# A two-layer decoder trunk: the modulation rows of the feed-forward stage go through GpSimd's DMA queue

## The chip, the cores and the metric

One core of one Trainium2 chip runs the whole kernel. The metric is device time in microseconds, as the median of several runs; beside it stands one execution taken with the hardware profiler. The engines are TensorE (PE, its weight loads PEld), VectorE (DVE), ScalarE (ACT), GpSimd (POOL) and SyncE (SP). SP does no arithmetic here: it issues DMA transfers, one after the other in a fixed order, and waits before each until its destination buffer is free.

## The reference

256 tokens of width 2048 pass through two layers. Each layer has a mixer (sliding-window attention beside an RWKV-7 recurrence, joined by one output projection) and a SwiGLU feed-forward, both with a modulation computed from a condition vector `c`:

```python
cond = jax.nn.silu(c)
for l in range(DEPTH):
    mod = (jnp.einsum('bd,de->be', cond, w_ada[l]) + b_ada[l]).reshape(B, N_MOD, 1, D_MODEL)
    sh_m, sc_m, gt_m, sh_f, sc_f, gt_f = [mod[:, i] for i in range(N_MOD)]
    u = x * (1 + sc_m) + sh_m
    ...
    mix = jnp.concatenate([y_attn, y_rwkv], axis=-1) @ w_out[l]
    x = layer_norm(DEEPNORM_ALPHA * x + gt_m * mix, ln1_w[l], ln1_b[l])
    u = x * (1 + sc_f) + sh_f
    gate, up = jnp.split(u @ w_gate_up[l], 2, axis=-1)
    ffn = (jax.nn.silu(gate) * up) @ w_down[l]
    x = layer_norm(DEEPNORM_ALPHA * x + gt_f * ffn, ln2_w[l], ln2_b[l])
```

All weights are float32 and are read from HBM once. `w_ada` is 2048 x 12288 per layer, `w_gate_up` 2048 x 11264 and `w_down` 5632 x 2048. The modulation is a product of one vector with a matrix, and does not depend on the tokens, so it can be computed at any time before its use.

## The kernel before, in words

**Weights.** `steps` brings the weights in chunks of 128 x 1024 floats (512 KB) into the tile `raw`, four buffers deep (L420 to L422). ScalarE rounds a chunk into `hi` (L430, three buffers), VectorE subtracts and gets the remainder `lo` (L431, two buffers). `stream` then multiplies each with TensorE, three products per block (L452, L453, L455), so that two reduced-precision parts give nearly full precision. A chunk of the feed-forward's main loop makes 12 matmuls of 512 columns.

**Modulation rows.** `ada_steps` computes 1024 values of one modulation. It reads 16 rows of blocks, 128 x 1024 floats each, into the tile `ast` (two buffers, L260 and L261), and VectorE multiplies each by a column of `cond` and adds it into `aacc` (L263 for the first, L265 for the others). Then two empty steps follow, and `ada_sums` adds over the partitions with eight TensorE transposes (L322) and ScalarE sums (L326). One such unit takes 19 steps; 20 units are to be done in a fixed list. Two of them go through another function, `ada_direct`, inside layer 0's mixer.

**How the two are interleaved.** After each chunk of weights `pump` adds `pace[0]` to a counter and takes a step of the list whenever the counter reaches one. In the feed-forward the pace is `AF_`, 0.75 steps a chunk in layer 0. `need` takes steps at once where a value is required. Each multiply of a row is ordered behind the low part of the chunk before it (`anchor`, L266 and L267). The order of the instructions within each engine is laid out when the kernel is built, from this program order and a model of durations, and then is fixed.

**Feed-forward.** `channel` first finishes the output projection and the first LayerNorm. From L1260 on it runs two rounds: gate and up for six (then five) blocks of 512 hidden columns, and the down projection of what these blocks made, added into `z`. After the second round come the second LayerNorm and, in layer 0, the start of the next layer's mixer. A LayerNorm's inverse root is a power on GpSimd (`rstd`, L1130). In the feed-forward GpSimd does nothing else. In the mixer it has small work of its own, and issues 32 transfers for a triangular inverse (L790 and L793).

All other transfers, weights and modulation rows alike, are issued by SP through `dma = nc.sync.dma_start`, apart from twelve issued by ScalarE.

Of the kernel before, what the change touches and what calls it, by code (L numbers as in the profile page):

```python
# [69 lines left out]
def hybrid_trunk_kernel(  # L70
# [8 lines left out]
    V, S, G, PE = nc.vector, nc.scalar, nc.gpsimd, nc.tensor  # L79
    dma = nc.sync.dma_start  # L80
# [170 lines left out]
    def ada_steps(l, mod, c0):  # L251

        src = w_ada[l].rearrange("(j p) n -> p j n", p=P)
        n0 = mod * D + c0
        if direct[0]:
            yield from ada_direct(l, mod, c0, src[:, :, n0:n0 + 1024])
            return
        acc = adap.tile([P, 1024], F32, tag="aacc", name="aacc")
        for j in range(KT):
            t = adap.tile([P, 1024], F32, tag="ast", name="ast", bufs=2)  # L260
            dma(t, src[:, j, n0:n0 + 1024])  # L261
            if j == 0:
                V.tensor_scalar_mul(acc, t, cond[:, 0:1])  # L263
            else:
                ins = V.scalar_tensor_tensor(acc, t, cond[:, j:j + 1], acc, ALU.mult, ALU.add)  # L265
                if anchor:  # L266
                    tc.add_manual_dep(ins.ins, anchor[0], order, reason="behind the weight stream")  # L267
            yield
        for _ in range(LAG):
            yield  # L270

        ada_sums(l, mod, c0, [acc[:, i * P:(i + 1) * P] for i in range(8)])
        done.add((l, mod, c0 // 1024))
        yield

    def ada_direct(l, mod, c0, src):

        gv = ps.tile([P, 512], F32, tag="m0", name="gv", bufs=1)
        turn[:] = 1, 0
        ahead = []  # L280

        def row_sums(j):
            t = ahead.pop(0)
            for q in range(4):
                PE.matmul(gv[32 * q:32 * q + 32, 0:T], lhsT=cond[:, j:j + 1].to_broadcast([P, 32]), rhs=t[:, q * T:(q + 1) * T],
                          start=(j == 0), stop=(j == KT - 1))

        for j in range(KT):
            if j >= LAG:
                row_sums(j - LAG)  # L290
            t = adap.tile([P, 1024], F32, tag="aacc", name="ast") if j % 3 == 2 else adap.tile([P, 1024], F32, tag="ast", name="ast", bufs=2)
            dma(t, src[:, j])
            ahead.append(t)
            yield
        for j in range(KT - LAG, KT):
            row_sums(j)
            yield
        row = adap.tile([P, T], F32, tag="aacc", name="grow")
        S.copy(row, gv[:, 0:T])
        turn[:] = 1, 1  # L300
        b = bank()
        for i in range(2):
            PE.transpose(b[:, i * P:(i + 1) * P], row[:, i * P:(i + 1) * P], ident)
        col = mod * KT + c0 // P
        bv = b[:, 0:T].rearrange("p (i q r) -> p q i r", q=4, r=32)
        V.scalar_tensor_tensor(mods[l][:, col:col + 8].rearrange("p (q i) -> p q i", q=4), bv[:, :, :, 0], 1.0 if mod in (1, 4) else 0.0,
                               prm(l, "b_ada", col, 8).rearrange("p (q i) -> p q i", q=4), ALU.add, ALU.add)
        done.add((l, mod, c0 // 1024))
        yield

    def ada_sums(l, mod, c0, blocks, idle=0):

        col = mod * KT + c0 // P
        n = len(blocks)
        sm = adap.tile([P, 8], F32, tag="asum", name="asum", bufs=2)
        for q in range(0, n, 4):
            b = bank()
            if q == 0:
                warm(b, idle)
            m = min(4, n - q)  # L320
            for i in range(m):
                PE.transpose(b[:, i * P:(i + 1) * P], blocks[q + i], ident)  # L322
            for i in range(m):
                bi = b[:, i * P:(i + 1) * P]
                if RED:
                    S.activation(bi, bi, AF.Copy, accum_out=sm[:, q + i:q + i + 1])  # L326
            if not RED:
                V.reduce_sum(sm[:, q:q + m], b[:, 0:m * P].rearrange("p (i k) -> p i k", k=P), axis=AX.X)
        V.scalar_tensor_tensor(mods[l][:, col:col + n], sm[:, 0:n], 1.0 if mod in (1, 4) else 0.0,
                               prm(l, "b_ada", col, n), ALU.add, ALU.add)  # L330
        if mod in (2, 5):
            row = adap.tile([8, P], F32, tag="arow", name="arow", bufs=2)[0:n]
            rb = bank()
            PE.transpose(rb[0:n, 0:P], mods[l][:, col:col + n], ident)
            S.copy(row, rb[0:n, 0:P])
            dma(gates[l, mod // 3, c0 // P:c0 // P + n], row)
# [23 lines left out]
    def ada_all(units):  # L360
        for l, m, h in units:
            yield from ada_steps(l, m, h * 1024)
# [10 lines left out]
                       + halves(1, 5))  # L373
    pace = [0.0, 0.0]
    anchor = []
    direct = [False]

    def pump():

# [101 lines left out]
    def cols(w, c0, width):  # L481
        wv = w.rearrange("(k p) n -> p k n", p=P)

        def f(rv, k0, m):
            return [(rv, wv[:, k0:k0 + m, c0:c0 + width])]
        return f
# [646 lines left out]
    def normalise(fp, z, t, stt):  # L1133
        mv, rs = rstd(fp, stt)
        V.scalar_tensor_tensor(rs[:, 1:2], mv[:, 0:1], -1.0, rs[:, 0:1], ALU.mult, ALU.mult)
        for q in range(4):
            zq = z[:, t, q * 512:(q + 1) * 512]
            if q % 2:
                S.activation(zq, zq, AF.Identity, scale=rs[:, 0:1], bias=rs[:, 1:2])
            else:  # L1140
                V.tensor_scalar(zq, zq, rs[:, 0:1], rs[:, 1:2], ALU.mult, ALU.add)
# [38 lines left out]
    def channel(l, ys, wa, fp):  # L1180
# [31 lines left out]
        for c0, w in ((1024, 512), (1536, 512)):  # L1212
            nq = w // 512
            bk = all_banks(nq)
            src, pieces = cols(w_out[l], c0, w), [(q * 512, 512) for q in range(nq)]
# [34 lines left out]
        def finish(t):  # L1250
            mv, rs = rstd(fp, stt[t])
            V.tensor_scalar_mul(mv[:, 0:1], mv[:, 0:1], -1.0)
            for q in range(4):
                o = q * 512
                zq = z[:, t, o:o + 512]
                V.scalar_tensor_tensor(zq, zq, mv[:, 0:1], lw[:, o:o + 512], ALU.add, ALU.mult)
                V.scalar_tensor_tensor(zq, zq, rs[:, 0:1], lb[:, o:o + 512], ALU.mult, ALU.add)
                dma(out[0, t * P:(t + 1) * P, o:o + 512], zq)

        gtf = fp.tile([P, D], F32, tag="gt", name="gtf")  # L1260
        wg = w_gate_up[l].rearrange("(k p) (s n) -> p k s n", p=P, s=2)
        first = True
        for lo_g, hi_g in ((0, 6), (6, 11)):
# [42 lines left out]
            for c0, w in ((0, 1024), (1024, 512), (1536, 512)):  # L1306
# [11 lines left out]
                for ts in ((0,), (1,)) if apart else ((0, 1),):  # L1318
# [5 lines left out]
                    for t in ts:  # L1324
# [8 lines left out]
                        if c0 == 1536 and not first:  # L1333
                            finish(t) if l + 1 == L else normalise(fp, z, t, stt[t])
            first = False
        if l + 1 == L:
            return None, None
        us = []
# [44 lines left out]
    for l in range(L):  # L1383
        pace[0] = AP[l]
        with tc.tile_pool(name=f"mix{l}", bufs=1, reuse_waits="tile") as mp:
            ys, wa = mixer(l, us, mp, feeds)
        pace[0] = AO[l]
        with tc.tile_pool(name=f"ffn{l}", bufs=1, reuse_waits="tile") as fp:
            us, feeds = channel(l, ys, wa, fp)
# [30 lines left out]
```

## Time and profile before

| | us |
|---|---|
| median of 3 runs | 2661.34 |
| lowest and highest run | 2660.47, 2666.17 |
| profiled execution | 2673.23 |
| its span, first to last instruction | 2671.2 |
| busy: PE, DVE, ACT, POOL | 2514.0, 1804.7, 1186.5, 146.7 |

The profiled execution is one more run, with the profiler on. Rows of the profile give an instruction's engine, source line, operation and tiles (`out<-in`), how often it occurs, and its time. A window's row gives each engine's busy time in that stretch, the clock that TensorE was granted (1.00 is full speed), the mean busy share of the 16 DMA engines, and the bytes moved. A wait's row says which instruction stood still for what, with the total, the number of times and the longest. The chain of waits follows the work that ended last back through what released it.

### The profile page before, as it was taken

What the parts mean: (1) busy time and instruction counts of PE and PEld (TensorE: products, weight loads), DVE (VectorE), ACT (ScalarE), POOL (GpSimd) and SP (SyncE); (2) the same over time, 40 slices, a digit from 0 to 9 for tenths busy, and PEclk for the clock granted to TensorE, in tenths of its full rate; (3) what the DMA queues carried; (4) which work ended last, traced back from release to release, by engine and by line L of the source; (5) the groups of instructions that cost most, each with busy time, mean ns of one, the idle gap of its engine ahead of it and who ended that gap; (6) DMA issues with size and microseconds to landing.
All of it is one profiled execution on the core that took longest, in us unless ns stands there. A gap on an engine that the chain in (4) does not pass through costs nothing.

```text
span 2671.2 us, 42267 instructions
## 1 busy us (share of the span) xinstructions
PE 2514.0 (94%) x15619; PEld 2090.1 (78%) x15619; DVE 1804.7 (68%) x2439; ACT 1186.5 (44%) x2023; POOL 146.7 (5%) x368
## 2 busy tenths in 40 slices
PE   3799998999999999999999998989899999999997
PEld 3697785677878888888788977867788888888887
DVE  7977766579877777677787776564855455545456
ACT  2464454435544444444454644543444443344442
POOL 1002212000000000000000024110000000000000
PEclk9899998999999999999999999988999999999999
DMA  9978658698998889888878785414655655566654
GB/s 371 358 215 253 202 176 266 207 335 301 327 328 303 309 301 317 284 299 304 293 247 291 218 264 148 129 50 179 221 189 184 195 184 196 195 190 188 191 189 149
DMA packets 336384, 637.51 MB, mean 239 GB/s; under 512 B 59510, under 2 KB 126514, under 8 KB 334642
## 3 DMA queue, kind: packets, MB, share of 16 engines
q1 hardware_dynamic: 333170, 629.05, 71.0%
q0 software_dynamic: 1280, 2.62, 0.4%
q10 hardware_dynamic: 1728, 3.15, 0.3%
q8 instruction: 122, 2.00, 0.3%
q14 instruction: 84, 0.69, 0.1%
HBM read 622.08 MB, written 12.62 MB: 238 GB/s over the span
## 4 chain that ended last, share of the span: by engine, by line
PE 62%; DMA 6%; DVE 5%; ACT 1%; issue 1%; POOL 0%; SPq 0%; DVEq 0%; ACTq 0%; POOLq 0%
PE acc L453 18%; PE acc L455 17%; PE acc L452 17%; DMA ast<-in_w_ada_dram 3%; DVE lo L431 2%; PE acc L465 1%; PE acc L466 1%; PE acc L464 1%; DMA raw<-in_w_gate_up_dram 1%; DVE aacc L265 1%; PE mb L1290 1%; DMA raw<-in_w_out_dram 1%; DMA raw<-in_w_in_dram 1%; PE mb L322 0%; DMA tm<-tinv 0%
## 5 line engine op out<-in xcount | busy, mean ns | idle before, releaser
L430 ACT CAST hi<-raw 128x1024 fp32r<-128x1024 f32 (+2 forms) x728 | 758.2, 1044 | 1093.2 <-PE acc L455 826.5
L431 DVE TENSOR_TENSOR lo<-raw,hi 128x1024 fp32r<-128x1024 f32 (+2 forms) x728 | 880.4, 1212 | 519.0 <-PE acc L453 350.1
L453 PE MATMUL acc<-lo,u 128*128 128x512 f32 x1568 | 515.7, 396 | 14.3 <-DVE lo L431 14.3
L455 PE MATMUL acc<-hi,u 128*128 128x512 f32 x1568 | 508.1, 392 | 0.0
L452 PE MATMUL acc<-hi,u 128*128 128x512 f32 x1568 | 460.1, 395 | 0.7 <-ACT u L410 0.7
L265 DVE SCALAR_TENSOR_TENSOR aacc<-ast,cond,aacc 128x1024 f32<-128x1024 f32 x270 | 345.7, 1280 | 105.8 <-DMA ast<-in_w_ada_dram 104.5
L453 PEld LDWEIGHTS acc<-lo,u 128*128 128x128 f32 x1568 | 294.2, 189 | 80.2 <-DVE lo L431 20.1
L452 PEld LDWEIGHTS acc<-hi,u 128*128 128x128 f32 x1568 | 296.3, 189 | 63.3 <-issue 1.2
L455 PEld LDWEIGHTS acc<-hi,u 128*128 128x128 f32 x1568 | 296.3, 189 | 61.9 <-issue 0.3
L453 PE MATMUL acc<-lo,ht 128*128 128x512 f32 (+1 forms) x720 | 243.7, 377 | 3.4 <-DVE lo L431 3.0
L455 PE MATMUL acc<-hi,ht 128*128 128x512 f32 (+1 forms) x720 | 242.2, 375 | 0.0
L452 PE MATMUL acc<-hi,ht 128*128 128x512 f32 (+1 forms) x720 | 217.1, 376 | 0.0
L464 PE MATMUL acc<-u,hi 128*128 128x256 f32 x720 | 201.1, 287 | 1.8 <-ACT hi L430 1.8
L465 PE MATMUL acc<-u,hi 128*128 128x256 f32 x720 | 201.3, 287 | 0.0
L466 PE MATMUL acc<-u,lo 128*128 128x256 f32 x720 | 188.7, 289 | 1.9 <-DVE lo L431 1.7
L453 PEld LDWEIGHTS acc<-lo,ht 128*128 128x128 f32 x720 | 135.1, 188 | 30.2 <-DVE lo L431 6.4
L455 PEld LDWEIGHTS acc<-hi,ht 128*128 128x128 f32 x720 | 135.6, 188 | 24.2
L452 PEld LDWEIGHTS acc<-hi,ht 128*128 128x128 f32 x720 | 134.8, 188 | 24.4
L464 PEld LDWEIGHTS acc<-u,hi 128*128 128x128 f32 x720 | 139.8, 194 | 4.5 <-ACT hi L430 2.0
L465 PEld LDWEIGHTS acc<-u,hi 128*128 128x128 f32 x720 | 139.6, 194 | 2.9 <-issue 1.6
L466 PEld LDWEIGHTS acc<-u,lo 128*128 128x128 f32 x720 | 130.7, 194 | 6.5 <-DVE lo L431 3.3
L1130 POOL TENSOR_TENSOR brs<-brs,mhalf 128x1 f32<-128x1 f32 x8 | 7.3, 916 | 1711.9 <-DVE brs L1129 776.6
(358 smaller groups left out, 2923.6 us busy)
## 6 DMA issues: line engine op xcount, KB each, us to landing
ast<-in_w_ada_dram SPq DMA_DIRECT2D x368, 512.0 KB
raw<-in_w_gate_up_dram SPq DMA_DIRECT2D x704, 256.0 KB
raw<-in_w_down_dram SPq DMA_DIRECT2D x176, 512.0 KB
raw<-in_w_in_dram SPq DMA_DIRECT2D x82, 512.0 KB
raw<-in_w_out_dram SPq DMA_DIRECT2D x64, 512.0 KB
raw<-in_w_in_dram SPq DMA_DIRECT2D x120, 256.0 KB
ast<-in_w_ada_dram SPq DMA_DIRECT2D x32, 256.0 KB
lnw<-in_ln_w_dram SPq DMA_DIRECT2D x4, 1024.0 KB
```

The costliest lines, as they stand in the source:

```text
L265: ins = V.scalar_tensor_tensor(acc, t, cond[:, j:j + 1], acc, ALU.mult, ALU.add)
L430: S.copy(h, fl)
L431: ins = V.tensor_tensor(r, fl, h.bitcast(F32), ALU.subtract)
L452: PE.matmul(bt, lhsT=xh, rhs=hi[:, c0:c0 + w], start=st, stop=False)
L453: PE.matmul(bt, lhsT=xh, rhs=lo[:, c0:c0 + w], start=False, stop=False)
L455: PE.matmul(banks[t][q][:, 0:w], lhsT=xl, rhs=hi[:, c0:c0 + w], start=False, stop=sp_)
L464: PE.matmul(bt, lhsT=hi[:, c0:c0 + w], rhs=xh, start=st and opens, stop=False)
L465: PE.matmul(bt, lhsT=hi[:, c0:c0 + w], rhs=xl, start=False, stop=False)
L466: PE.matmul(bt, lhsT=lo[:, c0:c0 + w], rhs=xh, start=False, stop=sp_ and closes)
L1130: G.tensor_tensor(rs[:, 0:1], rs[:, 0:1], mhalf[:, 0:1], ALU.pow)
L1290: PE.transpose(b[:, i * T + t * P:i * T + (t + 1) * P], hh[t][:, (2 * k2 + i) * P:(2 * k2 + i + 1) * P], ident)
```

## The change

A flag `quiet` is set just before the feed-forward's two rounds are laid out and is cleared after them. While it is set, `ada_steps` issues its transfers from GpSimd (`G.dma_start`) and not from SP. The transfers themselves, their buffers and all arithmetic stay the same, and so do the weights' issues. `ada_direct` and `ada_first` are not touched. The flag is set in both layers.

```diff
         for j in range(KT):
             t = adap.tile([P, 1024], F32, tag="ast", name="ast", bufs=2)
-            dma(t, src[:, j, n0:n0 + 1024])
+            (G.dma_start if quiet[0] else dma)(t, src[:, j, n0:n0 + 1024])
...
-    direct = [False]
+    direct, quiet = [False], [False]
...
         gtf = fp.tile([P, D], F32, tag="gt", name="gtf")
+        quiet[0] = True
         wg = w_gate_up[l].rearrange("(k p) (s n) -> p k s n", p=P, s=2)
...
             first = False
+        quiet[0] = False
         if l + 1 == L:
             return None, None
```

## The prediction, made before the change was run

> **What bounds the kernel now.** I read the page first, then the two feed-forward stages as windows, then the waits inside the first one, then its chain of waits and its timeline.
>
> ```profile
> span 2671.2 us, 42267 instructions
> ...
> q0 software_dynamic: 1280, 2.62, 0.4%
> ```
>
> The profiled execution took 2673.23 us, 2.0 us more than its span and 11.9 us (0.45%) more than the median of the runs shown, 2661.34 us. I make the sum as a difference on the profiled execution and put it on the median.
>
> ```profile
> 621.00:1381.50 760.50, 751.91 (x3494) 622.12 (x3495) 585.59 (x583) 345.03 (x532) 0.54 (x1) 1.00 0.89 306
> 1921.50:2657.50 736.00, 735.97 (x3400) 614.11 (x3400) 388.30 (x415) 308.25 (x347) 1.62 (x2) 1.00 0.58 185
> ```
>
> The columns are the stretch, its length, then the busy time and count of PE, PEld, DVE, ACT and POOL, the granted clock, the DMA share and GB/s. The first row is the feed-forward of layer 0, from its first gate matmul to its last down matmul; the second is the same work in layer 1. Both are PE's. Modulation rows run only in the first:
>
> ```profile
> L261 SPq DMA_DIRECT2D ast<-in_w_ada_dram x175: 327/328/750, 618.4 to 1378.0; - x175
> L265 DVE SCALAR_TENSOR_TENSOR aacc<-ast,cond,aacc x164: 1272/1280/1287, 617.1 to 1376.7; 128x1024 f32<-128x1024 f32 x164
> ```
>
> So 175 transfers change queue, all in layer 0; by layer 1's feed-forward no row is left. Layer 0's stage is 24.5 us longer. Part of that is TensorE's work for the row sums:
>
> ```profile
> L322 PE MATMUL mb<-ident,aacc x88: 271/272/273, 665.2 to 1366.9; 128*128 128x128 f32 x88
> ...
> 1366.15 1.03 PE L322 MATMUL mb<-ident,aacc 128*128 128x128 f32 x8
> ```
>
> Eleven groups of eight at 1.03 us are 11.3 us. What remains, 24.5 - 11.3 = 13.2 us, is what PE loses to late weights there. That is all that a better order of transfers can win: 0.5%.
>
> ```profile
> ACT hi L430 <- PE acc L455: 321.4, 195, 4.9
> DVE aacc L265 <- DMA ast<-in_w_ada_dram: 65.3, 48, 4.0
> DVE lo L431 <- PE acc L453: 48.5, 36, 2.3
> ...
> ACT hi L430 <- DMA raw<-in_w_gate_up_dram: 37.4, 18, 5.4
> ...
> ACT hi L430 <- DMA raw<-in_w_down_dram: 14.3, 6, 2.8
> ```
>
> These are the waits of layer 0's stage (total us, times, longest). VectorE makes the low parts of the weights and multiplies the rows, in one order fixed at build time. When a row is late, VectorE stands (65.3 us in 48 waits, 1.36 us each) and the next low part is late. How little reserve it has shows against layer 1, where the same wait for PE, VectorE being ahead, is 275.8 us and not 48.5:
>
> ```profile
> DVE lo L431 <- PE acc L453: 275.8, 187, 1.7
> ```
>
> **The change part by part.** First, SP loses 175 issues of 0.328 us, 57 us. The question is whether weights wait behind a row on SP.
>
> ```profile
> 1330.30 1.21 DVE L431 TENSOR_TENSOR lo<-raw,hi 128x1024 fp32r<-128x1024 f32 x1
> 1339.61 1.28 DVE L265 SCALAR_TENSOR_TENSOR aacc<-ast,cond,aacc 128x1024 f32<-128x1024 f32 x1
> 1343.35 1.29 DVE L265 SCALAR_TENSOR_TENSOR aacc<-ast,cond,aacc 128x1024 f32<-128x1024 f32 x1 [1.32 <-DMA ast<-in_w_ada_dram]
> ...
> 1331.54 0.37 SPq L422 DMA_DIRECT2D raw<-in_w_down_dram  x1
> 1337.99 0.34 SPq L261 DMA_DIRECT2D ast<-in_w_ada_dram  x1
> 1340.92 0.34 SPq L261 DMA_DIRECT2D ast<-in_w_ada_dram  x1
> ```
>
> A low part ends at 1331.51 and frees a raw buffer; SP issues the next weights at 1331.54. A row's multiply ends at 1340.89 and SP issues the next row at 1340.92. SP is a follower of VectorE: it sits in wait and reacts in 0.03 us.
>
> ```profile
> SPq L422 <- DVE lo L431: 291.6, 246, 3.7
> ```
>
> Its weights wait 291.6 us for low parts. Taking the rows off SP is worth nothing by this; were a weight issue really held up now and then, it is at most the 0.33 us of one row's issue.
>
> Second, POOL gains 175 issues. The kernel has transfers on that queue already, in the mixer:
>
> ```profile
> L793 POOL DMA_DIRECT2D tm<-tinv x16: 682/687/702, 237.6 to 1749.5; - x16
> ...
> tm<-tinv POOLq DMA_DIRECT2D x16, 128.0 KB, 3.6
> ```
>
> An issue takes 0.69 us there against 0.33 on SP, so 175 are 121 us of POOL, which does 0.54 us of other work in the stage. Hidden. What they are queued ahead of is the power (L1130) of the LayerNorm that closes the stage, with VectorE and then PE behind it: at worst one issue, 0.7 us, once. The sixteen issues lie within 682 to 702 ns, so nothing that VectorE does meanwhile holds them up.
>
> Third, and this is the term that counts, the landing of a row. A row's slot is freed by the multiply two rows back, and its transfer starts then. How long it takes now is seen where the chain runs through it:
>
> ```profile
> 735.95 6.39 DMA ast<-in_w_ada_dram
> ...
> 1095.51 4.91 DMA ast<-in_w_ada_dram
> ...
> 1337.99 5.26 DMA ast<-in_w_ada_dram
> ...
> 1344.66 5.45 DMA ast<-in_w_ada_dram
> ```
>
> The mean is 5.5 us. What time it has follows from PE's pace:
>
> ```profile
> 661.69 0.91 PE acc L452 x4
> 664.41 0.91 PE acc L452 x4
> ```
>
> One weight chunk is 2.72 us. At the pace of 0.75 there are three rows in four chunks, so two rows further is 5.44 us or 8.16 us, and less the 1.28 us of the multiply a transfer has 4.16 or 6.88 us. At 5.5 us the short third of them waits 1.34 us: 173 multiplies / 3 = 58 waits of 1.34 us, against the 48 of 1.36 us that the trace has. The model holds, and it has two edges: below 4.16 us no row waits, above 6.88 us every row does.
>
> Now the landing on POOL's queue. The only rows are the mixer's 128 KB transfers, under three loads of the DMA engines:
>
> ```profile
> L793 POOL DMA_DIRECT2D tm<-tinv x2: 687/688/690, 441.1 to 441.8; - x2
> DMA to landing us min/median/max: 4.8/5.2/5.5
> L793 POOL DMA_DIRECT2D tm<-tinv x2: 682/686/689, 1559.3 to 1560.0; - x2
> DMA to landing us min/median/max: 6.8/6.9/6.9
> L793 POOL DMA_DIRECT2D tm<-tinv x2: 687/688/690, 1677.8 to 1678.5; - x2
> DMA to landing us min/median/max: 3.1/3.1/3.1
> ...
> 441.00:447.00 6.00, 5.61 (x51) 2.92 (x50) 2.89 (x11) 1.23 (x4) 3.06 (x3) 1.00 1.04 283
> 1559.00:1567.00 8.00, 7.46 (x59) 6.74 (x57) 5.44 (x10) 6.54 (x18) 1.90 (x3) 1.00 0.99 278
> 1677.00:1682.00 5.00, 5.00 (x56) 4.68 (x56) 1.52 (x2) 2.49 (x9) 1.67 (x3) 1.00 0.45 133
> ```
>
> The second last number is the DMA share: 3.1 us at 0.45, 4.8 to 6.9 us at about 1. A queue of its own does not escape the load. A row has 512 KB; at the 391 GB/s that the trace reaches at its best,
>
> ```profile
> 50.00:100.00 50.00, 37.58 (x278) 35.17 (x279) 47.10 (x48) 17.02 (x35) 0.00 (x0) 0.91 1.05 391
> ```
>
> the other 384 KB add 1.0 us. So the ends for a row are 4.1 us (unloaded) and 7.9 us (loaded); the stage's share of 0.89 is nearest to the loaded rows, which give 5.8 to 7.9. I take 6.5, below their middle because those transfers are cut into pieces of 256 bytes and a row into pieces of 4 KB. That is 1.0 us more than now.
>
> Then the 48 waits become 2.36 us each, +48 us, and some of the 6.88 us rows start to wait; I put +10 us on them. VectorE idles in all 760.5 - 585.6 = 175 us of the stage, 65 of it in these waits, so +58 us fits on the average and reaches PE only where waits come in a bunch. Now 65.3 + 37.4 + 14.3 = 117 us of late data cost PE 13.2 us, a share of 0.11; as reserve shrinks the share grows, and I take 0.17: 58 x 0.17 = +10 us. Sum: 0 (SP) + 0 to 0.7 (POOL) + 10 = 2673 + 10 = 2683 us profiled, 2671 on the median.
>
> The order in which the build lays out each engine's instructions may shift with the queue, and no row shows this: -5 to +5 us, taken as 0.
>
> The Trainium skill (DMA: Bandwidth & Descriptors, section "Latency and other measured facts") gives about 1 us to the first byte for a transfer issued by GpSimd and about 0.6 us by SyncE; by that the landing grows by 0.4 us as an estimate, 48 x 0.4 x 0.17 = 3 us, and the sum would be 2665. The loaded rows say more, and I go by them.
>
> **The rivals.** (a) No change that can be told. A row lands at up to 6.0 us on the new queue, because large pieces suffer less than small ones. Then 48 x 0.5 x 0.17 = 4 us at most, and VectorE's idle time takes it: 2661 to 2665, say 2663. For it speak SP's reaction in 0.03 us (nothing to win) and the 175 us of idle VectorE; against it the 4.8 to 6.9 us under load.
>
> The Trainium skill has a rule for this rival (same page, "Issuing engines are not separate DMA queues"): transfers of all issuing engines run on the same 16 DMA engines, and another issuer only saves sequencer time. The trace agrees so far as that POOL's transfers slow down with the load of SP's.
>
> (b) Faster. On its own queue a row passes the weights already queued on SP's, and lands at the unloaded 4.1 us. Below 4.16 us no row waits: the 65.3 us go, more than half of the 117 us of late data, and PE regains 65.3 / 117 x 13.2 = 7 us, up to 13 with the weights' share: 2648 to 2654. It decides from about 4.7 us on down, where half of the waiting is gone. For it speaks that a row now takes 5.5 us where size alone is 1.3 us, much of it in line; against it, that POOL's own small transfers were not spared the line.
>
> (c) Much slower. The landing is above 6.88 us, as the pair at 1559 would give. All 173 rows wait, VectorE has no reserve and becomes the bound: two rows per landing plus 1.28 us. At 7.5 us that is 4.39 us a row against 3.63 at the pace; 173 x 0.76 = 131 us of waits, of which the 110 us of VectorE's other idle time hide most: +20 to +45 us, 2681 to 2706.
>
> **How the numbers follow.** Forecast (landing 6.0 to 6.9 us, +6 to +20 us) 0.35; (a) 0.33; (b) 0.20; (c) 0.12. Of 2661.34 us, 0.2% is 5.3 us, about what a measurement tells from no change. Faster 0.20 is (b), same 0.33 is (a), slower 0.47 is the forecast and (c). The range leaves out the better half of (b) and the worse half of (c): 2652 to 2692. The forecast's own is 2667 to 2681.
>
> **What would show it.** Right: in the changed kernel's layer 0 stage the wait of L265 for the row's transfer is 100 to 140 us and not 65; SP's weights still go out within 0.05 us of a low part's end; POOL shows some 121 us of issues; the stage is about 770 us long against 760.5; layer 1's feed-forward stays at 736.0. Wrong for (b): the wait of L265 falls under 30 us and the stage under 755. Wrong for (c): nearly all 164 multiplies wait and PE's share in the stage falls below 0.97. And if the stages outside layer 0's feed-forward move by more than 5 us, it was the order of instructions, which I took as 0.

## The result, and the profile after

The changed kernel takes 2685.73 us against 2660.90 us of the kernel before on the same chip (medians of six runs each): 0.9% slower, ratio 1.009, 95% interval 1.007 to 1.011. The forecast was 2671 us in a range of 2652 to 2692, slower as the likeliest side. The direction came as predicted, and so did the chain behind it (late rows, late low parts, TensorE waiting). Why the rows are late and how much of it reaches TensorE did not, and the loss of 24.8 us is about two and a half times the +10 us of the sum.

The profiled execution of the changed kernel took 2685.16 us. First the page: the span, and the queues, where q0 is the one that GpSimd's issues go to (packets, MB, share of 16 engines).

```profile
span 2683.2 us, 42302 instructions
...
q1 hardware_dynamic: 308546, 539.39, 60.5%
q0 software_dynamic: 25904, 92.29, 10.4%
...
L261 POOL DMA_DIRECT2D ast<-in_w_ada_dram x171 | 90.4, 529 | 667.7 <-DVE aacc L265 527.9
...
ast<-in_w_ada_dram POOLq DMA_DIRECT2D x171, 512.0 KB, 5.6
```

q0 carried 2.62 MB before and carries 92.29 MB now: 171 rows of 512 KB are 89.7 MB more. Four of the 175 rows in the stage are those of the steps behind it and stay with SyncE.

Now the two feed-forward stages as windows, between the same matmuls as before (same columns: stretch, length, PE, PEld, DVE, ACT, POOL, clock, DMA share, GB/s).

```profile
624.50:1397.70 773.20, 755.91 (x3494) 621.06 (x3495) 584.36 (x583) 345.95 (x532) 90.94 (x172) 1.00 0.87 301
1932.50:2669.00 736.50, 735.81 (x3400) 613.70 (x3400) 388.14 (x415) 308.17 (x347) 1.62 (x2) 1.00 0.58 186
```

Layer 0's stage has grown from 760.5 to 773.2 us; layer 1's stands at 736.5 against 736.0. Outside layer 0's stage the two spans are level: 2671.2 - 760.5 = 1910.7 us before, 2683.2 - 773.2 = 1910.0 us after. PE's idle time in the stage (length less busy) went from 8.6 to 17.3 us, and its busy time from 751.9 to 755.9 at the same number of matmuls. The waits inside that stage (total us, times, longest):

```profile
DVE aacc L265 <- DMA ast<-in_w_ada_dram: 87.8, 57, 4.4
DVE lo L431 <- PE acc L453: 45.9, 34, 2.3
ACT hi L430 <- DMA raw<-in_w_gate_up_dram: 44.0, 21, 5.0
...
PEld acc L453 <- DVE lo L431: 29.4, 31, 2.7
...
PE acc L453 <- DVE lo L431: 17.0, 23, 2.3
ACT hi L430 <- DMA raw<-in_w_down_dram: 10.9, 5, 2.3
```

Rows are waited for 87.8 us and no longer 65.3. What follows from it stands in the last rows: PE and its weight loads wait longer for low parts. The same two waits in the kernel before:

```profile
PEld acc L453 <- DVE lo L431: 15.7, 18, 2.1
...
PE acc L453 <- DVE lo L431: 8.2, 13, 1.7
```

The weight load's wait has grown by 29.4 - 15.7 = 13.7 us, the stage by 12.7 us.

How late a row is shows in the timeline of the changed kernel.

```profile
1323.06 1.23 DVE L431 TENSOR_TENSOR lo<-raw,hi 128x1024 fp32r<-128x1024 f32 x1 [1.50 <-PE acc L453]
1324.31 0.38 SPq L422 DMA_DIRECT2D raw<-in_w_down_dram  x1
...
1326.92 1.28 DVE L265 SCALAR_TENSOR_TENSOR aacc<-ast,cond,aacc 128x1024 f32<-128x1024 f32 x1
...
1328.50 0.53 POOL L261 DMA_DIRECT2D ast<-in_w_ada_dram  x1 [2.19 <-DVE aacc L265]
```

SyncE still sends the weights 0.02 us after the low part (1323.06 + 1.23 = 1324.29). A row's multiply ends at 1328.20; GpSimd's issue begins at 1328.50 and takes 0.53 us, so it is over 0.83 us after the buffer came free. On SyncE it was over after 0.37 us (0.03 and 0.34). Each row's issue is over 0.46 us later; how this divides into a later start and a longer issue rests on GpSimd's spans, which are rough in the profile. Counted from the start of the issue it lands as before:

```profile
L261 POOL DMA_DIRECT2D ast<-in_w_ada_dram x171: 527/527/617, 624.9 to 1377.4; - x171
DMA to landing us min/median/max: 3.8/5.6/8.0
```

The median of 5.6 us is hardly more than the 5.5 us that the chain showed on SyncE's queue.

### The profile page after: what moved, and what is told of

Its sections match the earlier page's. It is cut to its first block, busy times and chain, and to the rows that moved or that the text cites. A ratio compares the mean times of both kernels' runs of the same rounds, so it can differ in the third digit from the quotient of the medians.

```text
span 2683.2 us, 42302 instructions
## 1 busy us (share of the span) xinstructions
PE 2521.1 (94%) x15619; PEld 2092.7 (78%) x15619; DVE 1803.5 (67%) x2439; ACT 1187.0 (44%) x2023; POOL 236.8 (9%) x539
## 3 DMA queue, kind: packets, MB, share of 16 engines
q0 software_dynamic: 25904, 92.29, 10.4%
## 4 chain that ended last, share of the span: by engine, by line
PE 73%; DMA 12%; DVE 8%; issue 2%; ACT 2%; POOL 1%; SPq 0%; DVEq 0%; POOLq 0%; ACTq 0%
PE acc L453 19%; PE acc L455 18%; PE acc L452 18%; DMA ast<-in_w_ada_dram 7%; DVE lo L431 3%; PE acc L466 3%; PE acc L465 3%; PE acc L464 2%; DVE aacc L265 2%; DMA raw<-in_w_out_dram 1%; DMA raw<-in_w_gate_up_dram 1%; PE mb L322 1%; PE mb L1291 1%; DVE aacc L353 1%; DMA tm<-tinv 1%
## 5 line engine op out<-in xcount | busy, mean ns | idle before, releaser
L430 ACT CAST hi<-raw 128x1024 fp32r<-128x1024 f32 (+2 forms) x728 | 758.4, 1044 | 1091.0 <-PE acc L455 823.9
L431 DVE TENSOR_TENSOR lo<-raw,hi 128x1024 fp32r<-128x1024 f32 (+2 forms) x728 | 880.2, 1212 | 507.9 <-PE acc L453 346.1
L453 PE MATMUL acc<-lo,u 128*128 128x512 f32 x1568 | 516.5, 397 | 19.0 <-DVE lo L431 18.9
L453 PEld LDWEIGHTS acc<-lo,u 128*128 128x128 f32 x1568 | 292.8, 189 | 87.6 <-DVE lo L431 27.9
L453 PE MATMUL acc<-lo,ht 128*128 128x512 f32 (+1 forms) x720 | 245.2, 379 | 6.3 <-DVE lo L431 6.2
L453 PEld LDWEIGHTS acc<-lo,ht 128*128 128x128 f32 x720 | 135.2, 189 | 34.6 <-DVE lo L431 11.0
L261 POOL DMA_DIRECT2D ast<-in_w_ada_dram x171 | 90.4, 529 | 667.7 <-DVE aacc L265 527.9
```

Of the source, the lines that this page charges most:

```text
L261: (G.dma_start if quiet[0] else dma)(t, src[:, j, n0:n0 + 1024])
L430: S.copy(h, fl)
L431: ins = V.tensor_tensor(r, fl, h.bitcast(F32), ALU.subtract)
L453: PE.matmul(bt, lhsT=xh, rhs=lo[:, c0:c0 + w], start=False, stop=False)
```

## The experiments

Theory 1: the rows come later, VectorE stands in line, the low parts come late and PE waits. Theory 2: transfers on the other queue take the DMA engines from the weights. A third possibility is that the build lays out another order of instructions when the queue changes. The quoted expectations name their rivals afresh: in `queue_alone` and `order_alone` theory 2 is the order.

**Queue or order.** The two sources give orders that differ in 17 places on ScalarE, 69 on PE and 50 on VectorE, all in layer 0's feed-forward. Two kernels cross them; each holds the three engines in the other kernel's order by scheduling dependencies alone, `PIN` being the list of instructions in that order:

```diff
+    held = {i.name: i for i in nc.cur_bb.bb.instructions}
+    for seg in PIN:
+        for p, n in zip(seg, seg[1:]):
+            tc.add_manual_dep(held[f"I-{n}"], f"I-{p}", order, reason="pinned")
```

`base` is the kernel before, `after_again` the changed one, `queue_alone` the changed one in the order of before, `order_alone` the kernel before in the order of the changed one.

> The kernel before, unchanged, for a second profile on the chip of the runs below. The two profiles at hand differ by 12 us, the medians by 25 us. Theory A (the whole loss lies in layer 0's feed-forward): this profile's stage is shorter than the first one's 760 us, about 748 to 755 us. Theory B (part of the loss lies elsewhere, in the mixer of layer 1): the stage is 760 us again and layer 1's mixer is shorter than the first one's 540 us. Time 2661 us, within 6.

> The changed kernel once more, with its two new statements put on lines that exist, so that line numbers equal those of before. 2686 us, +20 to +29 us against before, stage of layer 0's feed-forward 773 us, row waits of the multiply 85 to 90 us, by either theory.

> Rows on GpSimd's queue, but the order of the instructions of TensorE, VectorE and ScalarE is pinned to that of the kernel before. Theory 1 (the queue: each row lands later after its buffer is free, and VectorE stands in line for it): +18 to +25 us against before, row waits of 80 us or more. Theory 2 (the order that the build lays out with the other queue is worse): within 6 us of before.

> Rows on SP as before, but the order of the instructions of TensorE, VectorE and ScalarE is pinned to that of the changed kernel. Theory 1 (the queue): within 6 us of before, row waits of 60 to 70 us. Theory 2 (the order): +18 to +25 us against before.

Against the kernel before at 2661.51 us (in brackets the ratio and its 95% interval): `base` 2663.98 (1.0007, 0.999 to 1.0024); `after_again` 2680.68 (1.0066, 1.0042 to 1.009); `queue_alone` 2679.12 (1.0079, 1.0051 to 1.0107); `order_alone` 2659.36 (0.9994, 0.9976 to 1.0012). The queue carries the loss, and the order nothing that can be told. Layer 0's stage as a window, `queue_alone` and then `order_alone`:

```profile
615.80:1396.40 780.60, 759.26 (x3494) 623.17 (x3495) 583.49 (x583) 345.28 (x532) 90.97 (x172) 0.99 0.87 299
```

```profile
626.50:1382.10 755.60, 749.97 (x3494) 622.13 (x3495) 584.93 (x583) 345.71 (x532) 0.54 (x1) 1.00 0.89 308
```

Three traces with the rows on SyncE give 760.5 (the kernel before), 757.7 (`base`) and 755.6 us, mean 757.9; three with them on GpSimd 773.2 (the changed kernel), 776.7 (`after_again`) and 780.6, mean 776.8. The difference is 18.9 us, against a loss of 17.6 to 24.8 us in the medians. Outside the stage the spans are 1904.1 to 1916.3 us with the rows on SyncE and 1895.5 to 1911.5 us with them on GpSimd: no loss stands there. `base` falls between its own two theories (stage 757.7 us, layer 1's mixer 537.5), and the two kernels on GpSimd's queue are 0.4 and 0.8 us short of the loss expected of them.

**Half of the rows.** `(G.dma_start if quiet[0] and j % 2 else dma)(...)`.

> Every second row goes through GpSimd's queue, the others through SyncE's. Theory 1: each row pays its own 0.6 us, so about half of the loss: the wait for rows is 72 to 82 us, the stage some 767 us, 2667 to 2672 us in all. Theory 2: if a second queue beside SyncE's is what costs, by its mere presence, most of the loss is there with half the rows, 2674 us or more.

2668.21 us, 1.0036 (1.0018 to 1.0053), against 2660.11: +8.1 us, somewhat under half of the loss. Its stage, with 77.0 us of row waits (half of the increase):

```profile
619.10:1389.80 770.70, 756.17 (x3494) 623.21 (x3495) 584.91 (x584) 345.58 (x533) 45.54 (x86) 0.99 0.88 303
```

The loss falls with the number of rows moved, which speaks against the mere presence of a second queue.

**Four buffers.** If rows that come late are all of it, a row that is issued four multiplies ahead instead of two has the time. Rows `j % 4 > 1` get two more buffers in the feed-forward's pool, which `quiet[0]` now holds:

```diff
-            t = adap.tile([P, 1024], F32, tag="ast", name="ast", bufs=2)
+            t = quiet[0].tile([P, 1024], F32, tag="astf", name="ast", bufs=2) if quiet[0] and j % 4 > 1 else adap.tile(...)
```

> The rows stay with SyncE, but in layer 0's feed-forward they have four buffers instead of two, so a row's transfer starts four rows ahead of its use. If late rows are what the feed-forward pays for (theory 1), VectorE's wait for rows (62.5 to 65 us with two buffers) falls under 15 us, low parts are made earlier and the stage shortens from 757.5 us to 744 to 752 us: 2648 to 2660 us in all. If what counts is the load of the DMA engines (theory 2), more rows in flight make the weights later (ScalarE's waits for raw weights above 60 us), and the time stays or grows: 2661 to 2675 us.

> The same four buffers, with the rows on GpSimd's queue. Theory 1 (a row comes 0.6 us later from buffer to use, and VectorE stands in line): with four buffers 0.6 us is covered, the wait for rows falls under 20 us, and the kernel is level with the one with four buffers on SyncE's queue, within 5 us. Theory 2 (rows on a queue of their own take the DMA engines from the weights): the difference of about 19 us in the stage between the two queues stays, and ScalarE's waits for raw weights stay 10 us or more above those on SyncE's queue.

Both lost their row waits, and the stages were level: 749.7 us on SyncE's queue and 751.0 us on GpSimd's. The whole times were not: `before_b4` 2658.53 (0.9995, 0.998 to 1.0009), `after_b4` 2672.70 (1.005, 1.0032 to 1.0068). Two things other than the queue had changed with the buffers. The order drew row multiplies into the LayerNorm ahead of the stage. This is `before_b4` there, VectorE between the mean and the factor of the LayerNorm's second half:

```profile
617.11 1.28 DVE L265 SCALAR_TENSOR_TENSOR aacc<-ast,cond,aacc 128x1024 f32<-128x1024 f32 x1 [0.69 <-DMA ast<-in_w_ada_dram]
618.31 0.26 DVE L1127 BATCH_NORM_AGGREGATE bmv<-bst 128x2 f32<-128x24 f32 x1
618.48 1.23 DVE L265 SCALAR_TENSOR_TENSOR aacc<-ast,cond,aacc 128x1024 f32<-128x1024 f32 x1
619.63 0.15 DVE L1129 TENSOR_SCALAR brs<-bmv 128x1 f32<-128x1 f32 x1
...
622.27 1.54 PE L404 MATMUL mb<-ident,z 128*128 128x128 f32 x6 [9.39 <-DVE z L1141]
```

PE stands 9.4 us for it in one wait; in `base` it stands there twice, for 1.8 and 1.7 us. And `after_b4` had yet another order in layer 1's mixer. So the pair was run again, with PE, VectorE and ScalarE held in exactly the order of the kernel before:

> Four row buffers in layer 0's feed-forward, rows on SyncE's queue, and the instructions of PE, VectorE and ScalarE held in exactly the order of the kernel before. So only the buffers differ. Theory 1 (late rows cost the stage): no waits for rows, stage 745 to 752 us against 757.5, and nothing given back at the LayerNorm ahead of it as in the first kernel with four buffers: 2648 to 2657 us. If row waits were free on SyncE's queue, no change: 2661.

> The same as b4_sp with the rows on GpSimd's queue, the order again exactly that of the kernel before, so that the two differ in the queue alone. The first kernel with four buffers on GpSimd's queue was 14 us slower than its twin although its stage was as short; its order in layer 1's mixer was another. Theory 1: within 4 us of b4_sp, the 14 us were the order in the mixer. Theory 2 (the queue itself costs, through the DMA engines or through GpSimd): 10 to 20 us slower than b4_sp.

`b4_sp` took 2650.88 us, 0.9967 (0.9952 to 0.9981), `b4_pool` 2655.05 us, 0.9974 (0.996 to 0.9989), against 2660.54. Their intervals overlap (a difference of a few us between the two queues is not excluded), and both are faster than the kernel before. The stage of `b4_sp`, then of `b4_pool`:

```profile
615.60:1366.50 750.90, 747.51 (x3494) 621.92 (x3495) 587.06 (x585) 346.41 (x533) 0.54 (x1) 1.00 0.89 309
```

```profile
618.40:1369.40 751.00, 747.66 (x3494) 622.06 (x3495) 586.87 (x585) 346.38 (x533) 89.82 (x170) 1.00 0.89 309
```

And the waits of `b4_pool` around the stage:

```profile
ACT hi L430 <- DMA raw<-in_w_gate_up_dram: 41.0, 20, 4.7
...
ACT hi L430 <- DMA raw<-in_w_down_dram: 10.1, 5, 2.7
...
PEld acc L453 <- DVE lo L431: 6.0, 7, 1.6
...
PE acc L453 <- DVE lo L431: 3.3, 4, 1.1
...
DVE aacc L265 <- DMA ast<-in_w_ada_dram: 0.2, 1, 0.2
```

With 169 rows on GpSimd's queue and almost nothing waiting for them the loss is gone. That decides against theory 2: ScalarE's waits for weights are longer than in `b4_sp` (41.0 + 10.1 us against 26.0 + 7.7) and the stage is no longer. It also shows where the 14 us between `before_b4` and `after_b4` were: `b4_pool` differs from `after_b4` in the order alone and is 17.7 us faster. Layer 1's mixer takes 529.3 us in its trace and 547.5 in that of `after_b4`.

**Late rows on SyncE's queue.** Three attempts to make rows late without the other queue. In `rows_halves_sp` a row goes as two transfers of 512 columns:

> All rows stay with SyncE, but in layer 0's feed-forward each goes as two transfers of 512 columns, the second issued about 0.35 us after the first: a delay of a row by about 0.35 us on SyncE's own queue, with no work on GpSimd. Theory 1: VectorE's wait for rows grows to 75 to 85 us, and the time by more than half of the loss, +8 to +12 us: 2670 to 2674 us. Theory 2: nothing runs on the other queue, so no change, 2661 to 2664 us. If it is nearly as slow as the changed kernel, lateness alone is enough.

2661.21 us, 1.0004 (0.999 to 1.0018). It did not make rows late: over the waiting rows, from the end of the multiply that frees the buffer to the start of the next use, its trace has 5.84 us on average and that of `base` 5.82. The second half is issued later and is half as large. The miss says nothing on either theory.

In `late_sp` a row goes as three transfers, of 8, 8 and 112 partitions:

> Two row buffers and SyncE's queue as before, order held as before, but in layer 0's feed-forward each row goes as three transfers: 8, 8 and 112 partitions. The last and largest is issued two issue times, about 0.7 us, after the first, so a row is as late as on GpSimd's queue with nothing on that queue. Theory 1: VectorE's row waits 85 to 105 us, stage 772 to 782 us, 2674 to 2684 us in all. Theory 2: no more than 5 us slower than before.

2785.46 us, 1.047 (1.0449 to 1.0491), far outside both. Its stage, and two of its waits:

```profile
622.40:1499.40 877.00, 790.21 (x3494) 634.02 (x3495) 586.45 (x584) 344.44 (x533) 0.54 (x1) 0.97 0.96 266
```

```profile
ACT hi L430 <- DMA raw<-in_w_gate_up_dram: 213.0, 92, 6.8
DVE aacc L265 <- DMA ast<-in_w_ada_dram: 193.0, 103, 4.4
```

The DMA engines are busier (0.96 against 0.89) and move less (266 GB/s against 306), and the weights are late too. Rows cut in this way load the DMA engines more, so this run does not separate the theories.

In `late_mem` GpSimd clears 128 columns of the row's buffer, and SyncE's issue waits for that; bytes and queues stay as they are, and the order is held (`quiet[1]` is 2 inside the feed-forward only):

```diff
-            dma(t, src[:, j, n0:n0 + 1024])
+            (quiet[1] == 2 and G.memset(t[:, 0:128], 0.0), dma(t, src[:, j, n0:n0 + 1024]))
```

> Two row buffers and all transfers on SyncE's queue, order held as before. In layer 0's feed-forward GpSimd clears 128 columns of a row's buffer before its transfer is issued, so that SyncE's issue comes later by GpSimd's wake-up (about 0.3 us) and the clearing (0.2 to 0.3 us), and the bytes, pieces and queues of the DMA engines stay as they are. With 0.5 to 0.7 us this is the lateness that the rows have on GpSimd's queue. Theory 1 (lateness is all): row waits 85 to 100 us in 53 to 64 times, stage 770 to 780 us, 2673 to 2684 us in all. Theory 2 (the other queue): within 5 us of before.

2664.65 us, 1.0016 (0.9996 to 1.0035), against 2660.33. By the time alone this is what theory 2 expected, but the expected lateness of 0.5 to 0.7 us was wrong. Its timeline:

```profile
1326.97 1.27 DVE L265 SCALAR_TENSOR_TENSOR aacc<-ast,cond,aacc 128x1024 f32<-128x1024 f32 x1
...
1328.30 0.20 POOL L261 MEMSET ast<- 128x128 f32 x1 [3.32 <-DVE aacc L265]
1328.53 0.34 SPq L261 DMA_DIRECT2D ast<-in_w_ada_dram  x1
```

The multiply ends at 1328.24, GpSimd clears from 1328.30 to 1328.50, SyncE issues at 1328.53: 0.29 us after the buffer is free, 0.26 us more than before. For these 0.26 us the row waits are 75.3 us (62.5 in `base`) and the stage is 761.0 us, 3 us above the mean of 757.9. That fits theory 1 in sign and in the waits; the time by itself can't be told from no change.

Side by side, by the windows of each stage (one trace each, all in us but the last column). The second wait is ScalarE's for weights (the two rows of L430 from DMA); the third and the fourth are those of PE and of its weight loads for low parts (L453). The last column counts VectorE's row waits above 2.5 us, read from the timeline.

| kernel | row waits | ScalarE for weights | PE for low parts | PEld for low parts | stage | long row waits |
|---|---|---|---|---|---|---|
| `b4_sp` | 0 | 33.7 | 3.3 | 6.1 | 750.9 | 0 |
| `b4_pool` | 0.2 | 51.1 | 3.3 | 6.0 | 751.0 | 0 |
| `order_alone` | 57.3 | 26.7 | 5.3 | 11.0 | 755.6 | 4 |
| `base` | 62.5 | 33.3 | 6.9 | 13.4 | 757.7 | 4 |
| `rows_halves_sp` | 66.4 | 45.9 | 7.0 | 14.1 | 758.6 | 6 |
| kernel before | 65.3 | 51.7 | 8.2 | 15.7 | 760.5 | 7 |
| `late_mem` | 75.3 | 54.6 | 8.6 | 18.1 | 761.0 | 7 |
| `after_half` | 77.0 | 35.2 | 12.6 | 22.1 | 770.7 | 9 |
| changed kernel | 87.8 | 54.9 | 17.0 | 29.4 | 773.2 | 14 |
| `after_again` | 93.2 | 39.9 | 19.2 | 33.8 | 776.7 | 16 |
| `queue_alone` | 96.8 | 73.8 | 20.9 | 34.7 | 780.6 | 13 |

The stage follows the weight loads' wait for low parts: the stage less this wait is 742.9 to 745.0 us in all rows but `after_half` and `queue_alone` (748.6 and 745.9), the two with a granted clock of 0.99 and not 1.00. So what the change costs is PE standing for VectorE's low parts. ScalarE's waits for weights do not order the stages: `after_again` has less of them than the kernel before and is 16.2 us longer.

The first 62 us of row waits (mean of the three on SyncE: 61.7) cost 757.9 - 750.9 = 7 us of the stage, a share of 0.11. The next 31 us (mean on GpSimd: 92.6) cost 18.9 us, a share of 0.61.

## Why the prediction was right and wrong, step by step

**SyncE, 0: right.** The weights go out 0.02 us after a low part in the changed kernel as well; nothing was won by taking the rows away.

**GpSimd, hidden: right, the price too high.** An issue takes 0.53 us and not 0.69; 171 of them are 90.4 us and not 121, beside nothing that waits. With four buffers the same issues stand there, and the stage is as short as with SyncE's.

**The order, 0: right** for this change (`order_alone`, and 1910.7 against 1910.0 us outside the stage). That it can count is shown by `after_b4` against `b4_pool`. Layer 1's feed-forward stayed, as predicted.

**The landing, +1.0 us: mis-sized, and for the wrong reason.** The transfer itself lands in 5.6 us, not 6.5. What came instead is ahead of it: the issue is over 0.46 us later than on SyncE. From free buffer to use, the rows that are waited for take 5.76 to 5.84 us on average in three traces on SyncE's queue and 6.32 to 6.39 in three on GpSimd's, +0.5 us. From the end of the issue to the use they take 5.35 to 5.43 and 5.42 to 5.49 us: the same within 0.1. I had priced the landing from 128 KB transfers in pieces of 256 bytes under full load, and had left the issuing engine's own delay out. The row waits went up by 31 us and not by 58; at 87.8 to 96.8 us they stay below the 100 to 140 that I gave.

The estimate from the Trainium skill that I set aside (DMA: Bandwidth & Descriptors, "Latency and other measured facts": +0.4 us to the first byte) was the better price of the lateness. The traces show 0.46 us at the end of the issue; the first byte itself no trace here shows.

**The share that reaches PE, 0.17: the step that failed.** It is 0.61 for the added waits. I took the average share of the waits that were there (0.11) and raised it a little. That average is right for those: removing them all gains 7 us. But they had used up the slack that VectorE could give. Its own waits for PE (`DVE lo L431 <- PE acc L453`), in which it is ahead, are 83.3 and 82.4 us in `b4_sp` and `b4_pool`; the three traces with two buffers on SyncE's queue have 48.5 to 51.2 us, the three on GpSimd's still 45.5 to 49.2 us. The first 62 us of row waits came largely out of this reserve, the next 31 us hardly.

Whether it is the long waits that reach PE is open. `late_mem` and `after_half` have nearly the same total (75.3 and 77.0 us) and stages 9.7 us apart, and the second has 9 waits above 2.5 us against 7. But only 4.0 us of the 9.7 are PE's weight loads waiting, the clock of the second is 0.99 against 1.00, and the intervals of their whole times overlap.

So two errors met: 58 x 0.17 = 10 us was the sum, 31 x 0.61 = 19 us is what the traces have. They pull in opposite directions, and it was luck that the sum came as near as it did: with the waits right and the share as I had it, it would have been 31 x 0.17 = 5 us.

**The rivals.** Nothing speaks for (b): half of the rows took 5.6 us or more to land (the shortest 3.8), and the row waits rose where (b) has them under 30 us. (c) did not come: 57 of 162 multiplies wait, and PE's share of the stage is 0.978. As for (a), with two buffers the issuer's own time came on top of each row, and the kernel is slower; with four the two queues can't be told apart, 2650.88 and 2655.05 us. The rule of the Trainium skill (DMA: Bandwidth & Descriptors, "Issuing engines are not separate DMA queues": another issuer saves sequencer time and no more) agrees with that pair; it does not tell the result with two buffers.

**Open.** A lateness of 0.46 us on SyncE's queue was not reached without another disturbance. `late_mem` reached 0.26 us: its row waits are 13.6 us above the mean of the three on SyncE's queue and its stage 3.1 us, a share of 0.23 and not 0.61. So that lateness alone gives all of the 19 us is argued, not shown. What is shown is that the queue brings the loss, that the loss is PE standing for low parts, and that it goes when the rows have time.

## What to carry to other kernels

A transfer whose buffer is freed just in time carries the issuer's whole reaction: read from the timeline how long after the release the issue is over, on the old and on the new engine, before moving it. Price added waits at the margin and not by the average of those already there: where an engine's slack is spent, the next 31 us cost almost three times what the first 62 had cost. And when waits for a buffer are the loss, try more buffers before another queue: here four instead of two are worth 0.3% on either queue, provided that the order of the other work is held.

## What was not expected of the hardware

- In the profile GpSimd starts arithmetic 0.06 us after VectorE's release (the clearing in `late_mem`), but a DMA issue only after 0.30 us, and the issue then takes 0.53 us (512 KB) where SyncE reacts in 0.03 us and takes 0.33.
- A row cut into 8, 8 and 112 partitions drops the stage's rate from 306 to 266 GB/s at a higher DMA share (0.96), and costs 4.7% of the kernel (`late_sp`); cut into two halves of its columns it costs nothing that can be told (`rows_halves_sp`, 1.0004).
